# A gated encoder layer on one core: the FFN's row scale on the down product's sum, seven products in three accumulating chains, sums of weight blocks made by transfers that add

## The chip, the cores and the metric

The kernel runs on one core of a Trainium2 chip. The metric is the device time of one execution in microseconds (us); the runs before the change took 1766.96 to 1771.07, with a median of 1769.09. TensorE is called PE, VectorE DVE, ScalarE ACT, GpSimd POOL; SP issues most transfers.

## The reference, cut to what matters

The layer is computed for 1024 rows of a prompt and 32 rows of a sample with the same weights. Two attention mixers give `o_a` and `o_b`; then:

```python
def merge_and_ffn(x, o_a, o_b, gate_a, gate_b, w_branch_a, w_branch_b, w_out, g_ffn, w_up, w_down):
    pa = jnp.einsum('blc,cd->bld', o_a.reshape(B, L, WIDTH_A), w_branch_a)
    pb = jnp.einsum('blc,cd->bld', o_b.reshape(B, L, WIDTH_B), w_branch_b)
    m = jax.nn.sigmoid(gate_a) * pa + jax.nn.sigmoid(gate_b) * pb
    h = x + jnp.einsum('bld,de->ble', m, w_out)
    u = jnp.einsum('bld,df->blf', rmsnorm(h, g_ffn), w_up)
    return h + jnp.einsum('blf,fd->bld', jnp.square(jax.nn.relu(u)), w_down)
```

The model width is 1024, the FFN width 4096, everything is float32. `rmsnorm` divides a row by the root of its mean square (plus 1e-6) and multiplies by `g_ffn`. That divisor is one positive number for each row, so it can be applied before the relu, or, squared, after the down product.

## The kernel before, in words

All activations lie transposed: features on the 128 partitions, rows on the free axis. The 1056 rows are two groups: group one has rows 0 to 511 in one chunk of 512 columns, group two has rows 512 to 1055 in two chunks of 272. Each float32 operand is split into a high part in float32r (a cast on ACT) and the low rest (a subtraction on POOL or DVE), and a product is three matmuls (`three`): high by high, high by low, low by high.

A kernel written as one stream of operations is ordered by a planner (`Plan`). Each operation gets an estimated duration (`cost`), a rank (FAST 0, PREP 1, MAIN 2, FILL 3, SLOW 4) and its dependencies; the planner then steps through time and gives each engine the ready operation with the lowest rank and, within a rank, the earliest recorded one. The order on each engine's queue is fixed when the program is built; on the chip each engine runs its queue in order and waits on semaphores. FFN matmuls have rank FILL, the work that empties their PSUM banks FAST, the loading and splitting of weights PREP.

Weights come in units of 128 x 512 (four 128 x 128 blocks): a load into `wst`, the cast to `wh` on ACT, the subtraction to `wl` on POOL. Five `wh`/`wl` pairs are kept (`WB`).

The stages that matter here:

- `out` computes `h` block by block (`e`), scales it by `g_ffn` into the FFN's inputs `g.h` and `g.l`, adds up the squares in `g.acc`, and leaves `h` itself in `g.y`.
- `ffn_group` first turns `g.acc` into the row scale `rb2` (a matmul with ones to add over partitions, then `rsqrt` with a Newton step on DVE). 32 up blocks follow (`go_up`), in eight rounds `q` of four, each round followed by eight down blocks (`go_down(e, q)`), which are added to `g.y` block by block. The last up of a round comes one block early: four ups, among them the first of the next round, stand between two sets of downs.
- In group one an up block is one product of 24 matmuls of 512 columns, a down block one of 12. Ups and downs use the same ring of two PSUM banks (`pj`). Attention for later rows (`late`) runs beside the first half of group one's FFN.
- In group two an up step is a quad (`go_up_quad`): two up blocks by two column chunks, 2 x 2 x 2 products of half the depth, made with seven products (a Strassen-Winograd scheme) of 12 matmuls of 272 columns. Their operands are sums of quarters of the input (`quarters`) and of weight blocks (`quad_units`). The seven results lie in separate banks and are added on DVE. Group two has six `pj` banks for quads and two `pd` banks for downs.

After an up product the squared relu is made by DVE (`ru`: relu times the row scale, from PSUM to SBUF), POOL (`ru` squared), ACT (cast to `uh`, shown as `xh`) and DVE (the low part `ul`, shown as `xl`). The PSUM bank is free after the first of these.

The sums of weight blocks before, for blocks a11, a12, a21, a22 loaded into `raw` tiles:

```python
V.tensor_add(z, a21, a22)
s1 = part(z, w, "s", 4, V)
V.tensor_sub(a21, a11, a21)
V.tensor_sub(z, z, a11)
s2 = part(z, w, "s", 4, G)
s3 = part(a21, w, "s", 4, V)
V.tensor_sub(z, a12, z)
s4 = part(z, w, "s", 4, G)
```

All operations are recorded through one helper, so the profile shows one line (L408) for all; groups are told apart by tile names.

Of the kernel before, what the change touches and what calls it, by code (L numbers as in the profile page):

```python
# [19 lines left out]
D = 1024  # L20
# [82 lines left out]
class Plan:  # L103
# [115 lines left out]
    def cost(self, eng, op, out, ins, scalar, kw):  # L219
# [37 lines left out]
        if eng == ACT and op != "dma_start":  # L257
            d = 195 + 0.84 * n + (190 if "accum_out" in kw else 0)
            if op == "activation" and any(not isinstance(kw.get(k, 0.0), (int, float)) for k in ("scale", "bias")):
                d += 100  # L260
            return d - 90, d
        if eng == POOL:
            d = 300 + 0.9 * n if op in ("tensor_scalar", "memset") else 330 + 1.9 * n
            return d - 30, d
# [152 lines left out]
class Layer:  # L417
# [47 lines left out]
    def three(self, ps, wh, wl, xh, xl, first, last):  # L465

        mm = self.nc.tensor.matmul
        mm(ps, wh, xh, start=first, stop=False)
        mm(ps, wh, xl, start=False, stop=False)
        mm(ps, wl, xh, start=False, stop=last)  # L470

    def column_block(self, units, rhs, done, chunks, kn=KB, tag="pj"):

# [21 lines left out]
    def run(self):  # L495
# [23 lines left out]
        self.trir = c([128, 128], F32R, "trir")  # L519
        self.tri4r = c([128, DEC], F32R, "tri4r")  # L520
        self.gf = c([128, KB], F32, "gf")

        dt = lambda shape, name: nc.tile(self.dram, shape, F32, name)
        self.dq = dt([2 * H, 2, HD, T], "dq")
# [1 line left out]
        self.dv = dt([2 * H, 128, NT, 128], "dv")  # L526
        self.do = dt([2 * H, HD, T], "do")
        self.dg = dt([16, 128, T], "dg")

        self.wpool = nc.open("w")  # L530
        xp = nc.open("x")
# [112 lines left out]
    def constants(self):  # L644
        nc, a = self.nc, self.a
        for name, dst, n in (("tri", self.trir, 128), ("tri4", self.tri4r, DEC)):
            st = nc.tile(self.wpool, [128, 512], F32, name, tag="wst", bufs=3)
            nc.sync.dma_start(st[:, :n], a[name])
            nc.scalar.copy(dst, st[:, :n])
        nc.scalar.copy(self.identr, self.ident)  # L650
        nc.sync.dma_start(self.gf, a["g_ffn"])

    def normalise(self, sl):

# [665 lines left out]
    def out(self, g):  # L1320

        nc, a = self.nc, self.a
        for e in (0, 4, 1, 5, 2, 6, 3, 7) if g.i else range(KB):
            units = [self.unit(a["w_out"][e, j]) for j in range(2)]

            def done(c, cs, ps, e=e):
# [2 lines left out]
                    nc.sync.dma_start(xr, a["xT"][:, e, slice(g.lo + cs.start, g.lo + cs.stop)])  # L1329
                hv = g.y[:, e, cs]  # L1330
                nc.vector.tensor_add(hv, ps, xr)
                if g.i:
                    self.quarters(g, e, c, hv)
                if not g.i or c == 0 or e >= 4:
# [13 lines left out]
    def quarters(self, g, e, c, hv):  # L1348
# [32 lines left out]

    def quad_units(self, f):

        nc, a, w = self.nc, self.a, self.quads
        with nc.rank(PREP):
            raw = []
            for i, j in ((0, 0), (1, 0), (1, 1), (0, 1)):
                st = nc.tile(w, [128, 512], F32, "raw", bufs=10)
                nc.sync.dma_start(st, a["w_up"][f + i, j])
                raw.append(st)  # L1390
            a11, a21, a22, a12 = raw
# [9 lines left out]
            z = nc.tile(w, [128, 512], F32, "raw", bufs=10)  # L1401
            V.tensor_add(z, a21, a22)
            s1 = part(z, w, "s", 4, V)
            V.tensor_sub(a21, a11, a21)
            V.tensor_sub(z, z, a11)
            s2 = part(z, w, "s", 4, G)
            s3 = part(a21, w, "s", 4, V)
            V.tensor_sub(z, a12, z)
            s4 = part(z, w, "s", 4, G)
            p11 = part(a11, self.wpool, "w", WB, G)  # L1410
            p12 = part(a12, self.wpool, "w", WB, G)
            p22 = part(a22, self.wpool, "w", WB, G)
        return p11, p12, p22, s1, s2, s3, s4

    def ffn_group(self, g, late=iter(())):
        nc, a, i = self.nc, self.a, g.i
        rb2 = g.acc
        for c, cs in enumerate(g.chunks):
            ps = self.bank("pj")
            nc.tensor.matmul(ps[:, :g.n], self.ones, g.acc[c], start=True, stop=True)  # L1420
            with nc.rank(FAST):
                self.rsqrt(rb2[c], ps[:, :g.n], D, lambda n: g.tmp(n, "pb", 3))
        nq, us = DFF // 512, {}

        def go_up(f):
            units = [self.unit(a["w_up"][f, j]) for j in range(2)]
            us[f] = uh, ul = g.mh[:, f % 8], g.ml[:, f % 8]

            def done(c, cs, ps):
                r = g.tmp("ru", "pb", 3)  # L1430
# [5 lines left out]
            self.column_block(units, lambda k, cs: (g.h[:, k, cs], g.l[:, k, cs]), done, g.chunks)  # L1436

        def go_up_quad(f):

            a11, a12, a22, s1, s2, s3, s4 = self.quad_units(f)  # L1440
            for i in range(2):
                us[f + i] = g.mh[:, (f + i) % 8], g.ml[:, (f + i) % 8]
            n = g.n
# [3 lines left out]
            def product(w, xs):  # L1447
                ps = self.bank("pj")[:, :n]
                with nc.rank(FILL):
                    for k in range(4):  # L1450
                        ks = slice(k * 128, k * 128 + 128)
                        self.three(ps, w[0][:, ks], w[1][:, ks], *xs[k], k == 0, k == 3)
                return ps

            z = [nc.tile(self.op, [128, 2, n], F32, "part", tag="o32", bufs=4) for _ in range(2)]
            p1, u2, u3, u4 = z[0][:, 0], z[0][:, 1], z[1][:, 0], z[1][:, 1]
            add = nc.vector.tensor_add

            def done(i, c, ps):
                cs = slice(c * n, c * n + n)  # L1460
                uh, ul = us[f + i]
                r = g.tmp("ru", "pb", 3)
                nc.vector.scalar_tensor_tensor(r, ps, 0.0, rb2[c], op0=ALU.max, op1=ALU.mult)
                nc.gpsimd.tensor_mul(r, r, r)
                nc.scalar.copy(uh[:, cs], r)
                nc.vector.tensor_sub(ul[:, cs], r, uh.bitcast(F32)[:, cs])

            ps = product(a11, x(0, 0))
            with nc.rank(FAST):
                nc.scalar.copy(p1, ps)  # L1470
            p5 = product(s1, ta)
            ps = product(s2, tb)
            with nc.rank(FAST):
                add(u2, ps, p1)
                add(u4, p5, u2)
            ps = product(a12, x(1, 0))
            with nc.rank(FAST):
                add(ps, ps, p1)
                done(0, 0, ps)
            ps = product(s3, tc)  # L1480
            with nc.rank(FAST):
                add(u3, ps, u2)
                add(ps, ps, u4)
                done(1, 1, ps)
            ps = product(s4, x(1, 1))
            with nc.rank(FAST):
                add(ps, ps, u4)
                done(0, 1, ps)
            ps = product(a22, td)
            with nc.rank(FAST):  # L1490
                add(ps, ps, u3)
                done(1, 0, ps)
# [12 lines left out]
        done = 0  # L1505

# [114 lines left out]
```

## Time and profile before

| | us |
|---|---|
| median of three runs | 1769.09 |
| the three runs | 1766.96, 1769.09, 1771.07 |
| span of the profiled execution | 1767.0 |
| PE busy in the span | 1739.5 (98%) |
| DVE busy | 1175.5 (67%) |
| ACT busy | 932.7 (53%) |
| POOL busy | 1054.6 (60%) |

The profiled execution has no separately measured run time; its span goes from the first to the last instruction. The share of busy time is a mean over stages with different limits. Matmuls are pipelined, so a row of a matmul is longer than the distance from one to the next; that distance is read from a count in a stretch. Group one's FFN begins near 842 us and ends near 1295; group two's begins near 1391 and ends at 1764.

### The profile page before, as it was taken

The numbers are of one execution on the slowest core, as the hardware profiler recorded it, in microseconds if no ns is written. First come the engines' busy times: TensorE is split into PE (matmuls) and PEld (weight loads), VectorE is DVE, ScalarE is ACT, GpSimd is POOL, SyncE is SP. The second block draws the span as 40 slices with busy tenths as digits, with TensorE's granted clock in tenths as the row PEclk, the third lists the DMA queues.
The fourth block names the chain that finished last, engine by engine and source line by source line (L and its number), as shares of the span: only waits on it lengthen the run. The fifth ranks groups of instructions, "written<-read, shape, count | busy, mean of one in ns | idle before, by whom it ended". The sixth has DMA issues, their size and how long they took to land.

```text
span 1767.0 us, 32459 instructions
## 1 busy us (share of the span) xinstructions
PE 1739.5 (98%) x11394; PEld 1600.1 (91%) x11394; DVE 1175.5 (67%) x2427; ACT 932.7 (53%) x2007; POOL 1054.6 (60%) x901
## 2 busy tenths in 40 slices
PE   8999999999999999999999999999999999999999
PEld 7999999999899888888888888888899999999999
DVE  7555678999666645788975556333357897777764
ACT  7444598973255676766655545432236543333331
POOL 3623232435366574899875555675558986666663
PEclk9999999999999999999999999999999999999999
DMA  8244451544566668555254353433374333333312
GB/s 258 72 133 118 116 177 59 148 144 143 178 179 168 169 183 225 175 163 151 69 162 123 118 154 98 144 109 99 106 237 137 95 104 92 94 91 96 96 48 88
DMA packets 152851, 234.90 MB, mean 133 GB/s; under 512 B 27248, under 2 KB 54480, under 8 KB 152688
## 3 DMA queue, kind: packets, MB, share of 16 engines
q1 hardware_dynamic: 152256, 232.48, 45.8%
q8 instruction: 90, 1.47, 0.4%
q14 instruction: 73, 0.60, 0.1%
q10 hardware_dynamic: 432, 0.34, 0.1%
HBM read 182.58 MB, written 50.08 MB: 132 GB/s over the span
## 4 chain that ended last, share of the span: by engine, by line
PE 85%; DVE 6%; DMA 4%; POOL 3%; issue 1%; ACT 1%; SPq 0%; ACTq 0%; POOLq 0%; DVEq 0%
PE pj L408 53%; PE s L408 13%; PE pd L408 10%; PE t L408 4%; PE o L408 4%; DMA q<-dq 1%; POOL wl L408 1%; DVE xl L408 1%; DMA k<-dk 1%; DVE raw L408 1%; DVE acc L408 1%; DVE rw L408 0%; DMA o<-do 0%; SPq L408 0%; POOL acc L408 0%
## 5 line engine op out<-in xcount | busy, mean ns | idle before, releaser
L408 POOL TENSOR_TENSOR wl<-wst,wh 128x512 fp32r<-128x512 f32 x350 | 488.5, 1400 | 388.4 <-ACT wh L408 358.2
L408 PE MATMUL pj<-xh,wh 128*128 128x512 f32 (+1 forms) x1600 | 557.3, 348 | 0.6 <-DVE vt L408 0.3
L408 PE MATMUL pj<-xh,wl 128*128 128x512 f32 (+1 forms) x1600 | 557.4, 349 | 0.0
L408 PE MATMUL pj<-xl,wh 128*128 128x512 f32 (+1 forms) x1600 | 555.8, 348 | 0.0
L408 ACT CAST wh<-wst 128x512 fp32r<-128x512 f32 x350 | 216.8, 621 | 361.7 <-PE pj L408 222.0
L408 PEld LDWEIGHTS pj<-xh,wh 128*128 128x128 f32 x1600 | 301.1, 188 | 33.6 <-ACT xh L408 0.7
L408 PEld LDWEIGHTS pj<-xh,wl 128*128 128x128 f32 x1600 | 300.8, 188 | 32.7
L408 PEld LDWEIGHTS pj<-xl,wh 128*128 128x128 f32 x1600 | 301.0, 188 | 32.1
L408 PE MATMUL pd<-xh,wh 128*128 128x272 f32 x512 | 147.6, 288 | 2.0 <-DVE y L408 2.0
L408 PE MATMUL pd<-xl,wh 128*128 128x272 f32 x512 | 147.7, 288 | 0.0
L408 PE MATMUL pd<-xh,wl 128*128 128x272 f32 x512 | 147.6, 288 | 0.0
L408 DVE TENSOR_TENSOR xl<-ru,xh 128x272 fp32r<-128x272 f32 (+1 forms) x96 | 114.2, 1202 | 46.0 <-ACT xh L408 45.7
L408 DVE TENSOR_TENSOR tt<-t,tt 128x512 fp32r<-128x512 f32 (+2 forms) x168 | 100.2, 622 | 40.3 <-ACT tt L408 38.6
L408 DVE TENSOR_TENSOR_SCAN rem<-rem 128x896 f32<-128x896 f32 (+6 forms) x66 | 118.7, 1823 | 10.0 <-ACT rem L408 9.8
L408 POOL TENSOR_TENSOR p<-p,rem 128x895 f32<-128x895 f32 (+6 forms) x66 | 103.3, 1578 | 29.8 <-DVE rem L408 26.4
L408 ACT ACTIVATE junk<-score,cand 128x384 bf16<-128x384 f32 (+1 forms) x124 | 116.1, 936 | 9.3 <-DVE cand L408 7.0
L408 ACT CAST tt<-t 128x512 fp32r<-128x512 f32 (+2 forms) x168 | 84.8, 540 | 48.2 <-PE t L408 42.8
L408 DVE TENSOR_TENSOR y<-pj,y 128x512 f32<-128x512 f32 x72 | 49.6, 689 | 83.9 <-PE pj L408 83.8
L408 PE MATMUL s<-k,q 128*128 128x384 f32 (+5 forms) x384 | 95.7, 356 | 7.1 <-DMA k<-dk 2.5
L408 PE MATMUL s<-wl,xh 128*128 128x256 f32 (+1 forms) x360 | 101.8, 285 | 0.2 <-POOL wl L408 0.2
L408 PEld LDWEIGHTS o<-tt,v 128*128 128x128 f32 x640 | 93.0, 189 | 9.7 <-DVE tt L408 1.1
L408 PE MATMUL s<-wh,xh 128*128 128x256 f32 (+1 forms) x360 | 100.3, 286 | 0.9 <-DVE small L408 0.7
(245 smaller groups left out, 3963.6 us busy)
## 6 DMA issues: line engine op xcount, KB each, us to landing
wst<-w_down SPq DMA_DIRECT2D x128, 256.0 KB, 2.7
q<-dq SPq DMA_DIRECT2D x64, 256.0 KB, 5.2
wst<-w_up SPq DMA_DIRECT2D x64, 256.0 KB, 2.7
raw<-w_up SPq DMA_DIRECT2D x64, 256.0 KB, 2.8
k<-dk SPq DMA_DIRECT2D x48, 256.0 KB, 3.5
v<-dv SPq DMA_DIRECT2D x48, 256.0 KB, 3.7
wst<-w_g SPq DMA_DIRECT2D x42, 256.0 KB, 3.4
dv<-vs SPq DMA_DIRECT2D x32, 256.0 KB, 2.4
```

The lines of the kernel that those rows point to most:

```text
L408: fn(*args, **kw)
```

## The change

1. **Row scale.** `rb2` becomes the reciprocal of the mean square plus 1e-6, without root and Newton step, and is made behind the first up step (`scales`). The up products are no longer multiplied by it. After seven of the eight down rounds the sum in `g.y` is multiplied by `rb2` and `h` is added, both on POOL; the eighth round's product is multiplied by `rb2` on DVE and added. `h` is stored to DRAM by `out` (`dh`) and loaded back then (`hx`); the first down round is copied to `g.y` by ACT in place of an addition.
2. **Squared relu** (`square`): ACT relu from PSUM to SBUF, DVE product of the bank with it back into the bank, ACT cast from the bank, DVE subtraction from the bank.
3. **Quads.** The seven products run in three PSUM chains (px, pz, py) that go on accumulating after partial sums have been copied out by ACT (`keep`); signs of some operands are turned, with a negated `g_ffn` (`ngf`).
4. **Sums of weight blocks.** Four transfers a quad, issued by POOL, add a block from DRAM to a tile; a block can so be loaded more than once: nine transfers a quad in place of four. The low part of s2 moves from POOL to DVE. The planner counts 1000 ns for an issue on POOL.

The diff, cut to its core:

```diff
+        if op == "dma_start" and eng == POOL:
+            return 1000.0, 1000.0
...
+        nc.vector.tensor_scalar(self.ngf, self.gf, -1.0, None, op0=ALU.mult)
...  (out)
                 nc.vector.tensor_add(hv, ps, xr)
+                nc.sync.dma_start(self.dh[e, :, slice(g.lo + cs.start, g.lo + cs.stop)], hv)
...  (quarters)
+        neg = self.ngf[:, e:e + 1]
-            nc.scalar.activation(g.raw[-1][:, c * n:c * n + n], hv, AF.Copy, scale=gf)
-        def less(out, z):
-            nc.vector.scalar_tensor_tensor(out, hv, gf, z, op0=ALU.mult, op1=ALU.subtract)
+            nc.scalar.activation(g.raw[-1][:, c * n:c * n + n], hv, AF.Copy, scale=gf if e < 4 else neg)
+        def mix(out, by, op):
+            nc.vector.scalar_tensor_tensor(out, hv, by, out, op0=ALU.mult, op1=op)
-        less(t1, t1)
+        mix(t1, neg, ALU.subtract if e >= 4 else ALU.add)
-            less(t3, t3)
+            mix(t3, gf, ALU.subtract)
...  (quad_units)
+            def load(*blocks, out=None):
+                st = out
+                if out is None:
+                    st = nc.tile(w, [128, 512], F32, "raw", bufs=10)
+                    nc.sync.dma_start(st, src(*blocks[0]))
+                    blocks = blocks[1:]
+                for b in blocks:
+                    nc.gpsimd.dma_start(st, src(*b), accum_op=ALU.add)
+                return st
+            z = load((1, 0), (1, 1))
+            z3 = load((0, 0), (1, 0))
+            a11, a22, a12 = load((0, 0)), load((1, 1)), load((0, 1))
             s1 = part(z, w, "s", 4, V)
+            load((0, 0), out=z)
+            s2 = part(z, w, "s", 4, V)
+            load((0, 1), out=z)
+            s3 = part(z3, w, "s", 4, V)
             s4 = part(z, w, "s", 4, G)
...
+    def square(self, g, ps, uh, ul, sign=1.0):
+        nc = self.nc
+        r = g.tmp("ru", "pb", 3)
+        nc.scalar.activation(r, ps, AF.Relu, scale=sign)
+        nc.vector.scalar_tensor_tensor(ps, ps, sign, r, op0=ALU.mult, op1=ALU.mult)
+        nc.scalar.copy(uh, ps)
+        nc.vector.tensor_sub(ul, ps, uh.bitcast(F32))
...  (ffn_group)
-                self.rsqrt(rb2[c], ps[:, :g.n], D, lambda n: g.tmp(n, "pb", 3))
+        def scales():
+            for c in range(len(g.chunks)):
+                ps = self.bank("pj")
+                nc.tensor.matmul(ps[:, :n], self.ones, g.acc[c], start=True, stop=True)
+                with nc.rank(FAST):
+                    v = g.tmp("rv", "pb", 3)
+                    nc.vector.tensor_scalar(v, ps[:, :n], 1.0 / D, EPS, op0=ALU.mult, op1=ALU.add)
+                    nc.vector.reciprocal(rb2[c], v)
...  (go_up, done)
-                nc.vector.scalar_tensor_tensor(r, ps, 0.0, rb2[c], op0=ALU.max, op1=ALU.mult)
-                nc.gpsimd.tensor_mul(r, r, r)
-                nc.scalar.copy(uh[:, cs], r)
-                nc.vector.tensor_sub(ul[:, cs], r, uh.bitcast(F32)[:, cs])
+                              lambda c, cs, ps: self.square(g, ps, uh[:, cs], ul[:, cs]), g.chunks)
...  (go_up_quad)
+            px = product(a11, x(0, 0))
+            p1 = keep(px)
+            pz = product(s1, ta)
+            p5 = keep(pz)
+            product(s2, tb, px)
+            u2 = keep(px)
+            product(s4, x(1, 1), pz)
+            done(0, 1, pz, pz, u2)
+            py = product(a12, x(1, 0))
+            done(0, 0, py, py, p1)
+            product(s3, tc, px)
+            done(1, 1, self.bank("pj")[:, :n], px, p5)
+            product(a22, td, px)
+            done(1, 0, px, px)
...  (go_down, done)
-                nc.vector.tensor_add(g.y[:, e, cs], ps, g.y[:, e, cs])
-                if q == nq - 1:
-                    nc.sync.dma_start(self.o["yT"][:, e, slice(g.lo + cs.start, g.lo + cs.stop)], g.y[:, e, cs])
+                y = g.y[:, e, cs]
+                if q == 0:
+                    nc.scalar.copy(y, ps)
+                elif q < nq - 1:
+                    nc.vector.tensor_add(y, ps, y)
+                else:
+                    nc.vector.tensor_mul(ps, ps, rb2[c])
+                    nc.vector.tensor_add(y, ps, y)
+                    nc.sync.dma_start(self.o["yT"][:, e, slice(g.lo + cs.start, g.lo + cs.stop)], y)
+            if q == nq - 2:
+                for c, cs in enumerate(g.chunks):
+                    y = g.y[:, e, cs]
+                    with nc.rank(PREP):
+                        hx = nc.tile(self.op, [128, g.w], F32, "hx", tag="sg", bufs=3)[:, :n]
+                        nc.sync.dma_start(hx, self.dh[e, :, slice(g.lo + cs.start, g.lo + cs.stop)])
+                        nc.gpsimd.tensor_mul(y, y, rb2[c])
+                        nc.gpsimd.tensor_add(y, y, hx)
...
             go_up_quad(0)
+            scales()
             go_up_quad(2)
...
         go_up(0)
+        scales()
```

More of the change, by code (lines that the diff above doesn't have):

```diff
@@ L463, in rsqrt, with three @@
         nc.vector.tensor_mul(out, out, w)
-    def three(self, ps, wh, wl, xh, xl, first, last):
+    def three(self, ps, wh, wl, xh, xl, first, last, **kw):
         mm = self.nc.tensor.matmul
-        mm(ps, wh, xh, start=first, stop=False)
-        mm(ps, wh, xl, start=False, stop=False)
-        mm(ps, wl, xh, start=False, stop=last)
+        mm(ps, wh, xh, start=first, stop=False, **kw)
+        mm(ps, wh, xl, start=False, stop=False, **kw)
+        mm(ps, wl, xh, start=False, stop=last, **kw)
     def column_block(self, units, rhs, done, chunks, kn=KB, tag="pj"):
@@ L521, in run @@
         self.gf = c([128, KB], F32, "gf")
+        self.ngf = c([128, KB], F32, "ngf")
         dt = lambda shape, name: nc.tile(self.dram, shape, F32, name)
@@ L528, in run @@
         self.dg = dt([16, 128, T], "dg")
+        self.dh = dt([KB, 128, T], "dh")
         self.wpool = nc.open("w")
@@ L1385, in quad_units @@
         with nc.rank(PREP):
[L1386 to L1391, printed above, removed]
+            src = lambda i, j: a["w_up"][f + i, j]
+            def load(*blocks, out=None):
[7 more added lines that the diff above has]
+                return st
             def part(z, pool, tag, bufs, eng):
@@ L1400, in quad_units @@
             V, G = nc.vector, nc.gpsimd
-            z = nc.tile(w, [128, 512], F32, "raw", bufs=10)
-            V.tensor_add(z, a21, a22)
+            z = load((1, 0), (1, 1))
+            z3 = load((0, 0), (1, 0))
+            a11, a22, a12 = load((0, 0)), load((1, 1)), load((0, 1))
             s1 = part(z, w, "s", 4, V)
[L1404 to L1408, printed above, removed]
+            load((0, 0), out=z)
+            s2 = part(z, w, "s", 4, V)
+            load((0, 1), out=z)
+            s3 = part(z3, w, "s", 4, V)
             s4 = part(z, w, "s", 4, G)
@@ L1413, in quad_units @@
         return p11, p12, p22, s1, s2, s3, s4
+    def square(self, g, ps, uh, ul, sign=1.0):
[5 more added lines that the diff above has]
+        nc.vector.tensor_sub(ul, ps, uh.bitcast(F32))
     def ffn_group(self, g, late=iter(())):
         nc, a, i = self.nc, self.a, g.i
+        n = g.n
         rb2 = g.acc
[L1418 to L1421, printed above, removed]
-                self.rsqrt(rb2[c], ps[:, :g.n], D, lambda n: g.tmp(n, "pb", 3))
+        def scales():
[6 more added lines that the diff above has]
+                    nc.vector.reciprocal(rb2[c], v)
         nq, us = DFF // 512, {}
@@ L1427, in go_up @@
             us[f] = uh, ul = g.mh[:, f % 8], g.ml[:, f % 8]
-            def done(c, cs, ps):
-                r = g.tmp("ru", "pb", 3)
-                nc.vector.scalar_tensor_tensor(r, ps, 0.0, rb2[c], op0=ALU.max, op1=ALU.mult)
-                nc.gpsimd.tensor_mul(r, r, r)
-                nc.scalar.copy(uh[:, cs], r)
-                nc.vector.tensor_sub(ul[:, cs], r, uh.bitcast(F32)[:, cs])
-            self.column_block(units, lambda k, cs: (g.h[:, k, cs], g.l[:, k, cs]), done, g.chunks)
+            self.column_block(units, lambda k, cs: (g.h[:, k, cs], g.l[:, k, cs]),
+                              lambda c, cs, ps: self.square(g, ps, uh[:, cs], ul[:, cs]), g.chunks)
         def go_up_quad(f):
@@ L1442, in go_up_quad, with product @@
                 us[f + i] = g.mh[:, (f + i) % 8], g.ml[:, (f + i) % 8]
-            n = g.n
             ta, tb, tc, td = ([(th[:, k], tl[:, k]) for k in range(4)] for th, tl in g.sums)
             x = lambda j, c: [(g.h[:, 4 * j + k, c * n:c * n + n], g.l[:, 4 * j + k, c * n:c * n + n]) for k in range(4)]
-            def product(w, xs):
-                ps = self.bank("pj")[:, :n]
+            def product(w, xs, ps=None):
+                first = ps is None
+                if first:
+                    ps = self.bank("pj")[:, :n]
                 with nc.rank(FILL):
@@ L1451, in product @@
                         ks = slice(k * 128, k * 128 + 128)
-                        self.three(ps, w[0][:, ks], w[1][:, ks], *xs[k], k == 0, k == 3)
+                        self.three(ps, w[0][:, ks], w[1][:, ks], *xs[k], first and k == 0, k == 3, skip_group_check=True)
                 return ps
-            z = [nc.tile(self.op, [128, 2, n], F32, "part", tag="o32", bufs=4) for _ in range(2)]
-            p1, u2, u3, u4 = z[0][:, 0], z[0][:, 1], z[1][:, 0], z[1][:, 1]
-            add = nc.vector.tensor_add
@@ L1459, in done, with keep @@
-            def done(i, c, ps):
+            def keep(ps):
+                t = nc.tile(self.op, [128, g.w], F32, "part", tag="o32", bufs=4)[:, :n]
+                with nc.rank(FAST):
+                    nc.scalar.copy(t, ps)
+                return t
+            def done(i, c, out, ps, more=None):
                 cs = slice(c * n, c * n + n)
                 uh, ul = us[f + i]
[L1462 to L1492, printed above, removed]
+                with nc.rank(FAST):
+                    if more is not None:
+                        nc.vector.tensor_add(out, ps, more)
+                    self.square(g, out, uh[:, cs], ul[:, cs], -1.0 if i else 1.0)
+            px = product(a11, x(0, 0))
```

## The prediction

> **What bounds the kernel now.** I read the page first, then busy time by stretches, then the chain of waits, then groups of instructions.
>
> ```profile
> span 1767.0 us, 32459 instructions
> PE 1739.5 (98%) x11394; PEld 1600.1 (91%) x11394; DVE 1175.5 (67%) x2427; ACT 932.7 (53%) x2007; POOL 1054.6 (60%) x901
> PE 85%; DVE 6%; DMA 4%; POOL 3%; issue 1%; ACT 1%; SPq 0%; ACTq 0%; POOLq 0%; DVEq 0%
> ```
>
> TensorE (PE) is nearly always busy and carries 85% of the chain. The change removes no matmul, so it can only win time in which PE stands still. The stretches (start:end, length, then busy time and count of PE, PEld, DVE, ACT, POOL, granted clock, DMA share) say where that is.
>
> ```profile
> 842.00:1124.00 282.00, 281.39 (x1565) 244.74 (x1564) 184.42 (x376) 154.04 (x294) 166.18 (x126) 1.00 0.43 119
> 1127.00:1295.00 168.00, 168.00 (x743) 139.11 (x742) 52.34 (x62) 53.11 (x89) 107.01 (x85) 1.00 0.43 126
> ...
> 1360.00:1400.00 40.00, 39.63 (x308) 38.87 (x307) 32.38 (x39) 27.04 (x61) 40.00 (x40) 1.00 0.39 112
> 1400.00:1420.00 20.00, 17.66 (x128) 17.44 (x127) 20.00 (x34) 7.81 (x16) 14.20 (x13) 0.91 0.25 72
> 1420.00:1440.00 20.00, 19.19 (x146) 18.37 (x145) 19.57 (x34) 8.34 (x18) 16.75 (x14) 1.00 0.30 88
> 1440.00:1465.00 25.00, 24.11 (x192) 23.79 (x190) 25.00 (x38) 11.35 (x22) 21.37 (x18) 1.00 0.37 106
> 1465.00:1491.00 26.00, 25.57 (x201) 25.35 (x202) 17.82 (x34) 7.80 (x14) 14.85 (x14) 1.00 0.31 92
> 1491.00:1727.60 236.60, 236.60 (x1886) 236.60 (x1885) 165.78 (x299) 88.79 (x167) 160.01 (x136) 1.00 0.31 86
> 1727.60:1764.20 36.60, 36.08 (x288) 35.85 (x286) 14.36 (x29) 5.54 (x10) 11.40 (x10) 1.00 0.30 94
> ```
>
> From 1491 on, 1886 matmuls of 272 columns take 236.6 us, 0.1254 each without a gap: group two's FFN has nothing to win there. At that rate 1400 to 1491 holds 667 matmuls, 83.7 us of work in 91: **7.3 us are lost while group two's FFN opens** (3.9, 1.7, 0.9 and 0.8 by stretch), with DVE full. From 1127 to 1295 (group one's FFN alone, 512 columns) 743 matmuls take 168 us, 0.226 each: nothing is lost there either. The chain names the loss, and the clock adds to it:
>
> ```profile
> 1405.53 2.90 DVE acc L408 x2
> ...
> 1412.48 0.36 DVE ru L408
> 1412.84 0.04 issue
> 1412.88 8.07 PE pj L408 x50
> ...
> 1410.00:1413.00 3.00, 0.66 (x6) 0.44 (x5) 3.00 (x7) 0.03 (x1) 1.11 (x2) 1.00 0.31 70
> 1413.00:1416.00 3.00, 3.00 (x16) 3.00 (x17) 3.00 (x7) 1.69 (x4) 2.77 (x4) 0.61 0.38 120
> 1416.00:1419.00 3.00, 3.00 (x22) 3.00 (x21) 3.00 (x4) 1.03 (x3) 2.33 (x2) 0.82 0.48 163
> ```
>
> DVE works through the row scale (`acc`: reciprocal and Newton step) while all PSUM banks wait for `ru`, which multiplies by it. PE stops about 2.5 us, and the granted clock then is 0.61 and 0.82 for 6 us.
>
> **Part by part, group two.** Means are in ns, from 1491 to 1727.6:
>
> ```profile
> L408 POOL TENSOR_TENSOR wl<-wst,wh 128x512 fp32r<-128x512 f32 x43 | 56.2, 1307 | 66.0 <-ACT wh L408 66.0
> L408 DVE TENSOR_TENSOR xl<-ru,xh 128x272 fp32r<-128x272 f32 x41 | 49.9, 1235 | 4.5 <-ACT xh L408 4.5
> L408 DVE TENSOR_TENSOR y<-pd,y 128x272 f32<-128x272 f32 x81 | 33.7, 434 | 43.4 <-PE pd L408 43.4
> L408 POOL TENSOR_TENSOR ru<-ru 128x272 f32<-128x272 f32 x43 | 31.3, 736 | 0.9 <-DVE ru L408 0.9
> L408 POOL TENSOR_TENSOR sl<-raw,sh 128x512 fp32r<-128x512 f32 x20 | 30.3, 1515 | 0.0
> L408 DVE TENSOR_TENSOR raw<-raw 128x512 f32<-128x512 f32 x38 | 26.9, 708 | 0.3
> L408 ACT CAST sh<-raw 128x512 fp32r<-128x512 f32 x40 | 24.8, 620 | 12.3 <-PE pj L408 8.5 <-DVE raw L408 3.8
> L408 DVE TENSOR_TENSOR pj<-pj,part 128x272 f32<-128x272 f32 x43 | 18.8, 438 | 1.7 <-PE pj L408 0.7
> L408 ACT CAST xh<-ru 128x272 fp32r<-128x272 f32 x42 | 17.6, 418 | 8.1 <-POOL ru L408 8.0
> L408 DVE TENSOR_TENSOR sl<-raw,sh 128x512 fp32r<-128x512 f32 x20 | 16.3, 816 | 10.2 <-ACT sh L408 10.2
> L408 ACT COPY part<-pj 128x272 f32<-128x272 f32 x11 | 4.2, 379 | 0.0
> ```
>
> One period is a quad (84 matmuls) and four down blocks (96): 180 x 0.1254 = 22.6 us, 10.5 of them in that stretch. DVE has 15.8 us a period, ACT 8.5, POOL 15.3. After, on DVE: four weight sums go (4 x 0.708), PSUM additions fall from 7 to 3 (4 x 0.438), one split comes from POOL (+0.816), and the four low parts read PSUM beside one SBUF tile, like `y<-pd,y` (4 x (1.235 - 0.434) less): 15.8 - 2.8 - 1.8 + 0.8 - 3.2 = 8.8. On ACT: two more keeps (0.379) and four relus (like the 0.418 cast): 10.9. On POOL: 4 x 0.736 and 1.515 go, four transfer issues come: 10.8 + 4D. No row has an issue on POOL. I bound D by SP's issue below (0.33) and by POOL's own 1.5 us row; I take 1.3, the row of POOL's other work on such a tile: 16.0 of 22.6. Hidden; POOL binds only above D = 2.95.
>
> The sums become a chain: split s1, add, split s2, add, split s4. Each load lands after 2.8:
>
> ```profile
> raw<-w_up SPq DMA_DIRECT2D x64, 256.0 KB, 2.8
> L408 SPq DMA_DIRECT2D raw<-w_up x64: 327/328/543, 1299.2 to 1666.3; - x64
> DMA to landing us min/median/max: 2.5/2.8/6.5
> ```
>
> An adding transfer I bound by 2.5 and 6.5, and take 2.8, the median of the same 256 KB. Chain: 2 x (0.62 + 0.82) + 2 x (1.3 + 2.8) + 0.62 + 1.5 = 13.2 us, from the release of s1's buffer to s4 of the next quad. In steady state PE wants s4 one period and one product after that release, 22.6 + 1.5 = 24.1 us, so both adds together may be late by 11 us. In the opening, quad 2 follows quad 0 at once: 10.5 + 1.5 = 12.0. There the chain is 1.2 late, which a12 and s3 can fill (3 us), but POOL, in whose queue the adds stand, was full up to 1400 (40.00 of 40). What is queued behind a waiting add is POOL's splits of `wl`, and PE waits for those. So the opening: the scale moves behind quad 0 and shrinks to one reciprocal, nobody waits for it until the seventh down block; DVE falls well below full. I take back 5.3 of the 7.3 us and leave 2.0 for late adds (bounds: 0 and all 7.3).
>
> Hidden at nothing: the added stores and reloads of h (SP: 24 stores, 24 loads at 0.33; DMA share 0.25 to 0.43); 48 POOL operations on y, two for each of 24 pieces, in the seventh down block, where five weight buffers stand ahead and POOL had 66 us idle in the stretch shown; ACT's 24 copies for the first down block, five more 256 KB transfers a quad (4 + 4 x 256 KB a period become 9 + 4, a share of about 0.5); the one DVE operation that makes `ngf`; the sign changes, which replace operations one for one; group one's row scale, behind its first up, for which nobody waits. At the end one DVE multiplication stands before the last addition, which is exposed: **+0.45** (row `y<-pd,y`).
>
> **Part by part, group one.** Here ups and downs share two PSUM banks. Before, the bank of an up product was free after one DVE operation; after, it is read by relu, product, cast and subtraction. The step from the last up to the downs, alone on PE:
>
> ```profile
> 1191.85 0.62 ACT L408 CAST wh<-wst 128x512 fp32r<-128x512 f32 x1 [1.58 <-issue]
> 1192.03 0.69 DVE L408 SCALAR_TENSOR_TENSOR ru<-pj,acc 128x512 f32<-128x512 f32 x1 [0.31 <-PE pj L408]
> ...
> 1194.55 0.39 PE L408 MATMUL pj<-xh,wh 128*128 128x512 f32 x1
> ...
> 1194.75 0.69 DVE L408 TENSOR_TENSOR y<-pj,y 128x512 f32<-128x512 f32 x1 [2.03 <-PE pj L408]
> ...
> 1195.09 0.61 ACT L408 CAST xh<-ru 128x512 fp32r<-128x512 f32 x1
> ...
> 841.35 0.60 ACT L408 ACTIVATE p<-s 128x512 f32<-128x512 f32 x1
> ```
>
> The up ends at 1192.0; the first down runs in the other bank until 1194.55, where the second takes the up's bank. After: weight cast to 1192.47, relu (0.60) to 1193.07, product (0.69), cast (0.61), subtraction (0.69, a PSUM source) and 0.04 between engines: 1195.25. That is 0.7 late. If the planner rather runs the third down first, it waits for the first one's addition, 1194.75 + 0.69 + 0.05 = 1195.49: 0.95 late. I take 0.95. Between two ups there are 24 x 0.226 = 5.4 us, enough. The step comes eight times; four of them lie after 1124, without attention to fill in: **+3.8** (bounds 2.8 and 3.8). The other four lie beside attention: its matmuls fill some gaps, but DVE (184 of 282 us busy) and ACT put their own work between the four steps. Half price, 0.5 each: **+2.0** (bounds 0 and 6, a 1.5 us wait at each). POOL's squaring, which goes, lay off the path.
>
> **Sum.** -5.3 + 0.45 + 3.8 + 2.0 = +0.95 us on the profiled 1767.0, so 1768.0. The median of the runs, 1769.09, is 2.1 above that span; with the same distance: 1770.0. That is no change: 0.2% of this kernel, 3.5 us, is about what a measurement can tell.
>
> **Rivals.** *Faster*: the opening closes whole (-7.3), hand-overs cost only 0.7 (2.8) and nothing beside attention: -4.1, 1765.0; without any hand-over loss 1762.2. For it: DVE falls from 15.8 to 8.8. Against it: the second down needs the up's bank by construction. 27%.
>
> *Slower by held banks*: beside attention every step waits, 6 us: +5.0, 1774. It decides when those four steps cost over 4.6. For it: ACT and DVE are over half busy there. Against: attention has matmuls. 13%.
>
> *The opening stays shut*: adds and POOL's full queue take the place of the row scale, and 1 us is won, not 5.3: +5.2, 1774. For it POOL's 40.00 of 40; against it that the first two quads' blocks can be loaded far ahead (loads start at 1299). 9%.
>
> *POOL becomes the bound*: each 0.1 us of D above 2.95 costs 0.4 a period and 6 us over 15 periods; at 3.2, 1785. Against it: DVE's rows in the steady stretch are two-operand operations, which stretch POOL's own from 1307 to 1515 and no further. 7%.
>
> The Trainium skill, page SBUF — State Buffer, section SBUF: two separate sides, speaks for this last one: a transfer issued from GpSimd cannot get its descriptors written while VectorE runs a two-port mode, and one of about 0.62 us took 3.1. With D = 3.1, an estimate from that page, POOL would have 23.2 us a period and the kernel some 9 us more. No trace here shows such a transfer; the page ties the lock to copies and scalar operations, which the steady rows do not hold.
>
> The forecast itself holds the remaining 44%. Faster by over 0.2%: 27%; within: 44%; slower: 29%. The range, 1763.5 to 1778, cuts off POOL's case and the end of the faster one.
>
> **What would show it.** Right: 1400 to 1491 holds over 700 matmuls at clock 1.00; DVE near 8.8 a period; gaps near 0.9 at four steps from up to down after 1124, with PE waiting for DVE `xl` or `y`. Wrong: no such gaps; POOL over 20 us a period; an adding transfer landing after 9 us, with ACT `sh` waiting for it and PE for ACT.

## The result and the profile after

The changed kernel took **1786.16 us** (median; 1783.62 to 1789.47), the kernel before, run beside it, 1768.95. The ratio is 1.0098 [1.0083, 1.0113]: slower by 17 us. The forecast was 1770.0 in 1763.5 to 1778, so it was wrong, on the slow side.

The page of the changed kernel: span, busy engines, the software queue (packets, MB, share of 16 DMA engines), issues (KB, median us to landing), and the chain's shares.

```profile
span 1785.7 us, 32620 instructions
PE 1746.7 (98%) x11394; PEld 1601.3 (90%) x11394; DVE 1049.7 (59%) x2304; ACT 977.7 (55%) x2153; POOL 1026.9 (58%) x901
...
q0 software_dynamic: 9216, 16.78, 6.0%
...
PE 83%; DMA 5%; POOL 4%; DVE 4%; issue 2%; ACT 1%; SPq 0%; ACTq 0%; POOLq 0%; DVEq 0%
...
raw<-w_up POOLq DMA_DIRECT2D x64, 256.0 KB, 4.5
```

DVE lost 126 us of work and POOL 28, PE does the same 11394 matmuls, and the kernel is slower. The averages mislead: what counts is where PE stands still. I take that as **loss**: the length of a stretch less its matmuls at the spacing that they have without gaps. At 272 columns that is 0.1254 us, as counted in the prediction. For other widths I estimate (columns + 29)/2.4 ns from it, which gives 0.2254 us at 512, where 0.226 was counted, but take at least 0.108 us, the distance in runs of short matmuls, and four times as much for a row of the product with ones. The last is too much: two such rows and one matmul took 0.69 us at 1410.14, so a row takes 0.28, not 0.50, and the opening's losses are low by up to 0.9 us (by 0.4 in the kernel before). The table has us of the two profiled executions; its last stretch goes to 2.7 us before the end of the span, so it holds time behind the last matmul too.

| stretch | what runs | before | after | the steps summed to |
|---|---|---|---|---|
| 870 to 1124 | group one's FFN beside attention | 4.0 | 9.7 | +2.0 |
| 1124 to 1295 | group one's FFN alone | 0.6 | 6.4 | +3.8 |
| 1295 to 1395 | group two's branch and `out` | -0.3 | 3.0 | 0 |
| 1395 to 1495 | group two's FFN opens | 8.1 | 5.4 | -5.3 |
| 1495 to 1700 | group two's FFN, steady | 0 | 0 | 0 |
| from 1700 | its end | 0.6 | 6.9 | +0.45 |

The differences sum to 18.4 us; the spans differ by 18.7. Up to 780 us the change makes no difference of note (losses 40.3 and 40.8). By 1295 the changed kernel is some 12 us behind, so the same work lies later in it. Stretches of the changed kernel and then of the kernel before (columns as in the prediction; the last one is GB/s):

```profile
870.00:1124.00 254.00, 249.39 (x1378) 215.67 (x1377) 141.04 (x339) 142.19 (x271) 121.07 (x97) 1.00 0.44 122
1124.00:1295.00 171.00, 167.04 (x732) 136.40 (x731) 44.23 (x66) 61.51 (x105) 107.85 (x85) 1.00 0.42 122
1316.00:1326.00 10.00, 10.00 (x82) 10.00 (x81) 3.58 (x6) 2.94 (x5) 6.72 (x7) 1.00 1.03 302
1326.00:1336.00 10.00, 9.39 (x75) 9.17 (x74) 2.17 (x5) 3.45 (x6) 2.87 (x4) 1.00 1.08 313
1500.00:1700.00 200.00, 200.00 (x1596) 200.00 (x1595) 86.52 (x196) 90.69 (x197) 120.29 (x106) 1.00 0.67 150
1752.00:1757.00 5.00, 1.39 (x7) 0.95 (x6) 0.44 (x1) 0.00 (x0) 4.76 (x6) 0.93 0.11 28
1757.00:1760.00 3.00, 3.00 (x16) 3.00 (x15) 0.81 (x2) 0.62 (x1) 2.82 (x4) 0.54 0.54 143
```

```profile
870.00:1124.00 254.00, 253.47 (x1408) 220.86 (x1407) 157.42 (x352) 132.19 (x250) 145.94 (x115) 1.00 0.44 124
...
1306.00:1316.00 10.00, 10.00 (x82) 10.00 (x81) 10.00 (x12) 5.20 (x9) 6.46 (x5) 1.00 0.92 318
1316.00:1326.00 10.00, 10.00 (x82) 10.00 (x81) 5.42 (x13) 6.12 (x11) 7.39 (x7) 1.00 0.63 199
1326.00:1336.00 10.00, 10.00 (x82) 10.00 (x81) 5.62 (x11) 5.91 (x14) 9.27 (x11) 1.00 0.67 188
```

**Hand-overs in group one.** The timeline of the changed kernel at one of the four steps after 1124 (start, duration; in brackets the engine's idle time and what ended it):

```profile
1201.66 0.59 ACT L410 CAST xh<-pj 128x512 fp32r<-128x512 f32 x1 [0.77 <-DVE pj L410]
1202.25 0.39 PE L410 MATMUL pj<-xh,wl 128*128 128x512 f32 x1
1202.68 0.69 DVE L410 TENSOR_TENSOR y<-pj,y 128x512 f32<-128x512 f32 x1 [1.05 <-PE pj L410]
1203.29 0.68 DVE L410 TENSOR_TENSOR xl<-pj,xh 128x512 fp32r<-128x512 f32 x1
1203.42 0.50 PE L410 MATMUL pj<-xh,wh 128*128 128x512 f32 x1 [0.78 <-DVE y L410]
```

The up's bank is held by product, cast and subtraction (`xl`, until 1203.97), so PE turns to the other bank, which DVE's addition `y` releases: 0.94 more between two matmuls than their spacing. The four steps lose 0.95, 0.94, 0.94 and 1.03.

The largest stop beside attention, 1.86 us, is at a step of the same kind, from the last up of a round to its downs:

```profile
894.60 3.74 DVE L410 TENSOR_TENSOR_SCAN rem<-rem 128x1024 f32<-128x1024 f32 x1 [0.26 <-ACT rem L410]
...
899.45 0.59 ACT L410 COPY y<-pj 128x512 f32<-128x512 f32 x1
...
900.09 0.50 PE L410 MATMUL pj<-xh,wh 128*128 128x512 f32 x1 [1.70 <-ACT y L410]
```

The relu of the up's bank was done at 894.99, but DVE's product stands behind attention's scan `rem` and starts at 898.26; ACT's cast of the bank waits for the product, and behind the cast, in ACT's order, stands the copy `y` that frees the other bank for PE.

**The opening.** The chain of the changed kernel (start, us, what) no longer stops for the row scale's result near 1410, but twice later (`sh` and `sl` are the high and low part of a sum of weight blocks). Then DVE, POOL and ACT on the timeline:

```profile
1424.86 1.76 DVE acc L410
1426.91 2.21 DVE sl L410
1429.16 1.53 PE pj L410 x10
...
1442.92 0.88 POOL raw L410
1443.89 7.27 DMA raw<-w_up
...
1452.47 1.78 PE pd L410 x12
```

```profile
1424.18 0.68 DVE L410 TENSOR_TENSOR sl<-raw,sh 128x512 fp32r<-128x512 f32 x1
...
1426.83 2.27 DVE L410 TENSOR_TENSOR sl<-raw,sh 128x512 fp32r<-128x512 f32 x1
...
1425.72 2.83 POOL L410 TENSOR_TENSOR wl<-wst,wh 128x512 fp32r<-128x512 f32 x2
...
1451.23 0.62 ACT L410 CAST sh<-raw 128x512 fp32r<-128x512 f32 x1 [2.85 <-DMA raw<-w_up]
1452.03 0.39 ACT L410 COPY y<-pd 128x272 f32<-128x272 f32 x1
```

The first stop (2.13 us) is a split of a sum, `sl`, behind the reciprocal `acc` in DVE's order: the row scale still stands on this chain. The split takes 2.27 us in place of the 0.68 of the one before it, with two subtractions of POOL beside it until 1428.55. (The Trainium skill, page SBUF — State Buffer, section SBUF: two separate sides, calls the port pair that VectorE and GpSimd share an exclusive lock: an operation of VectorE with two SBUF inputs waits for the whole of one on GpSimd. The end of `sl` 0.55 us after POOL's agrees.) The second (1.71 us) is an adding transfer that lands after 7.27 us; ACT's cast `sh` waits for it, and behind that, in ACT's order, stands the copy of a down product whose bank PE needs. Two waits of the product with ones for POOL's sum of squares `acc`, at 1410 and 1415, take another 1.1 us (0.7 in the kernel before).

**The end.** PE and POOL of the changed kernel on the timeline:

```profile
1752.80 0.29 PE L410 MATMUL pd<-xl,wh 128*128 128x272 f32 x1
1756.42 0.60 PE L410 MATMUL pd<-xh,wl 128*128 128x272 f32 x1 [3.33 <-POOL wl L410]
...
1752.24 0.76 POOL L410 TENSOR_TENSOR y<-y,hx 128x272 f32<-128x272 f32 x1 [0.61 <-DMA hx<-dh]
1752.96 1.47 POOL L410 TENSOR_TENSOR y<-y,acc 128x272 f32<-128x272 f32 x2
1754.39 0.76 POOL L410 TENSOR_TENSOR y<-y,hx 128x272 f32<-128x272 f32 x1
1755.10 1.26 POOL L410 TENSOR_TENSOR wl<-wst,wh 128x512 fp32r<-128x512 f32 x1
```

Four operations on `y` stand ahead of the weight split `wl` for which PE waits 3.33 us, and the clock is 0.54 in the next 3 us (stretch above). In all 5.6 us are lost up to the last matmul; the rest of the 6.9 lies behind it, with the multiplication added there.

**The steady stretch** has no loss, as said: 1596 matmuls in 200.00 us.

### The profile page after: what moved, and what is told of

Same layout as the page of the kernel before. It is cut to its first block, busy times and chain, and to the rows that moved or that the text cites. A ratio compares the mean times of both kernels' runs of the same rounds, so it can differ in the third digit from the quotient of the medians.

```text
span 1785.7 us, 32620 instructions
## 1 busy us (share of the span) xinstructions
PE 1746.7 (98%) x11394; PEld 1601.3 (90%) x11394; DVE 1049.7 (59%) x2304; ACT 977.7 (55%) x2153; POOL 1026.9 (58%) x901
## 3 DMA queue, kind: packets, MB, share of 16 engines
q0 software_dynamic: 9216, 16.78, 6.0%
## 4 chain that ended last, share of the span: by engine, by line
PE 83%; DMA 5%; POOL 4%; DVE 4%; issue 2%; ACT 1%; SPq 0%; ACTq 0%; POOLq 0%; DVEq 0%
PE pj L410 51%; PE s L410 13%; PE pd L410 10%; PE t L410 5%; PE o L410 4%; POOL wl L410 2%; DMA sg<-dg 1%; DVE xl L410 1%; DMA raw<-w_up 1%; POOL y L410 1%; DMA q<-dq 1%; POOL xl L410 1%; POOL acc L410 1%; POOL pb L410 0%; SPq L410 0%
## 5 line engine op out<-in xcount | busy, mean ns | idle before, releaser
L410 POOL TENSOR_TENSOR wl<-wst,wh 128x512 fp32r<-128x512 f32 x350 | 483.4, 1389 | 390.4 <-ACT wh L410 365.4
L410 POOL TENSOR_TENSOR p<-p,rem 128x895 f32<-128x895 f32 (+6 forms) x66 | 99.2, 1516 | 32.2 <-DVE rem L410 29.8
L410 ACT CAST tt<-t 128x512 fp32r<-128x512 f32 (+2 forms) x168 | 84.7, 541 | 44.3 <-PE t L410 40.3
L410 PE MATMUL s<-wh,xl 128*128 128x256 f32 (+1 forms) x360 | 100.8, 283 | 0.0
L410 PE MATMUL o<-tt,v 128*128 128x256 f32 (+1 forms) x640 | 99.0, 278 | 1.4 <-DVE o L410 0.7
```

The costliest lines, as they stand in the source:

```text
L410: fn(*args, **kw)
```

## The experiments

Each ratio is to the kernel before, run beside it on the same chip, with its 95% interval.

**u1: the operations on y to DVE.**

```diff
-                        nc.gpsimd.tensor_mul(y, y, rb2[c])
-                        nc.gpsimd.tensor_add(y, y, hx)
+                        nc.vector.tensor_mul(y, y, rb2[c])
+                        nc.vector.tensor_add(y, y, hx)
```

> The changed kernel with the row scale of the sum and the addition of h moved from POOL to DVE. Theory P (48 operations on POOL, about 36 us, push the last weight splits back, and TensorE stops 3.5 us at 1752.8 and then runs at clock 0.54): the gap near the end and the one at 1267 in group one go, 5 to 7 us less than the changed kernel, so about 1780. Rival: the stop comes from late loads of weights or of h, then the gap stays and the time too (1786).

1782.5 us, 1.0069 [1.0057, 1.0081]: 5 us of the loss is back. At the end the loss falls from 6.9 to 3.6 (what is left are three waits for DVE's `y`, 1.29, 0.57 and 0.33 us, and the time behind the last matmul), and from 6.4 to 5.3 in 1124 to 1295, where the changed kernel had one wait of 0.89 at 1267 for POOL `wl` as well.

**u2: group one's up bank free after one operation.** Relu to SBUF as in the change, then the square on POOL, cast and subtraction from SBUF.

```diff
         nc.scalar.activation(r, ps, AF.Relu, scale=sign)
+        if not g.i:
+            nc.gpsimd.tensor_mul(r, r, r)
+            nc.scalar.copy(uh, r)
+            nc.vector.tensor_sub(ul, r, uh.bitcast(F32))
+            return
```

> The changed kernel, but in group one the squared relu works from the SBUF copy after ACT's relu (POOL squares, ACT casts, DVE subtracts), so the PSUM bank is free after one operation. Theory B (held banks): the four gaps of 0.95 after 1124 go, and most of the 5.8 us lost beside attention too: 6 to 9 us less, about 1778. Rival: the loss beside attention comes from another order of the attention work; then only the 3.8 us go, about 1782.

1778.41 us, 1.0043 [1.0026, 1.0060]. One edit takes 6.3 us out beside attention (9.7 to 3.4) and 4.0 after it (6.4 to 2.4); u2's stretch, to be held against the two above:

```profile
870.00:1124.00 254.00, 254.00 (x1415) 221.25 (x1414) 141.99 (x328) 144.24 (x276) 144.07 (x115) 1.00 0.43 124
```

So the held bank, with DVE's product on it, is the cause at both places, and beside attention it costs more than alone. Of the 2.4 left, 1.55 is one wait for POOL `wl`; in u2 the operations on y are still on POOL.

**u3: the sums of weight blocks on DVE again,** four loads a quad, s2's low part left on DVE.

```diff
-            z = load((1, 0), (1, 1))
-            z3 = load((0, 0), (1, 0))
-            a11, a22, a12 = load((0, 0)), load((1, 1)), load((0, 1))
+            a11, a21, a22, a12 = load((0, 0)), load((1, 0)), load((1, 1)), load((0, 1))
+            z = nc.tile(w, [128, 512], F32, "raw", bufs=10)
+            V.tensor_add(z, a21, a22)
+            V.tensor_add(a21, a11, a21)
+            z3 = a21
...
-            load((0, 0), out=z)
+            V.tensor_add(z, z, a11)
...
-            load((0, 1), out=z)
+            V.tensor_add(z, z, a12)
```

> The changed kernel with the sums of weight blocks made by DVE again (four additions of 128x512 a quad, four loads a quad), all else as in the changed kernel. Theory X (adding transfers cost: 7.3 us to land at 1443.9, ACT waits in order behind them, and their traffic slows the loads of group two's branch): losses at 1334, 1346 and 1450 go, 4 to 5 us less, about 1781.5. Rival (DVE relief by the transfers is worth more): DVE fills again in the opening, 2 to 4 us slower, about 1789.

1780.17 us, 1.0053 [1.0040, 1.0066]. The loss of 1295 to 1395 goes (3.0 to -0.1), the opening's falls from 5.4 to 3.6, now mostly one stop of 2.87 us for DVE's work on a bank of the quad (`pj`), after which the clock is 0.50 for 3 us. u3's stretches:

```profile
1316.00:1326.00 10.00, 10.00 (x82) 10.00 (x81) 5.99 (x12) 4.31 (x8) 4.83 (x4) 1.00 1.00 360
1326.00:1336.00 10.00, 10.00 (x82) 10.00 (x81) 6.29 (x11) 5.60 (x10) 6.69 (x6) 1.00 0.66 205
```

Here too the 16 DMA engines are full for ten us, but they move 360 GB/s and are through at 1326; in the changed kernel they move 302 and 313 and stay full until 1336. In the kernel before, 12 us earlier, they were 0.92 busy for ten us at 318 GB/s, with no loss.

**u4: the three together.**

> The three edits together: what is left of the change is the row scale on the sum, the three accumulating chains and, in group two, the squared relu in PSUM. If the three theories hold and add up: 1786 less 6, 8 and 4.5, about 1767; and since the opening's row scale is gone too, it may fall below the kernel before, to 1764. If they share one cause, it stays above 1772.

1765.84 us, 0.9978 [0.9970, 0.9987]: faster than the kernel before. The single edits took 0.0029, 0.0055 and 0.0045 off the ratio, 0.0129 in sum; together they take 0.0120. As far as the intervals tell, the three causes are separate and make up the whole loss; what is left of the change (scale on the sum, chains, group two's squared relu in PSUM) is a gain of 4 us.

**v1: u4, but the operations on y on POOL, recorded with the last rank.**

```diff
-                        nc.vector.tensor_mul(y, y, rb2[c])
-                        nc.vector.tensor_add(y, y, hx)
+                    with nc.rank(SLOW):
+                        nc.gpsimd.tensor_mul(y, y, rb2[c])
+                        nc.gpsimd.tensor_add(y, y, hx)
```

> As the kernel with all three edits (1765.8 against 1770.7 of the kernel before), but the 48 operations on y are on POOL again and ranked behind everything else there (SLOW in place of PREP); the loads of h keep their rank. If their place in POOL's queue was the fault: no stop near the end, nor the 2.2 us of gaps that DVE's operations on y make there, and 1.5 to 3 us less than with DVE, about 1763. Rival: POOL has not the time at all; then the stop of 3.5 us is back, about 1770.

1763.32 us, 0.9965 [0.9953, 0.9978]; loss from 1700 on: 1.1, against 3.6 in u4, and PE has no stop there (over all runs the intervals of v1 and u4 overlap). POOL has the time, here without the adding transfers; the rank PREP and the early place in the record put the work ahead of the splits.

**v2: u4 with 8 plain transfers more a quad,** of weights to memory that nobody reads.

```diff
+            for k in range(8):
+                nc.sync.dma_start(self.idle[f // 2 % 2 * 8 + k], src(k % 2, k // 2 % 2))
```

> As the kernel with all three edits, plus eight plain transfers of 256 KB a quad from the weights to an unused place in DRAM, issued by SP with the loads: about the time on the DMA engines that the adding transfers took, without POOL's issue, without a chain and without anyone who waits for them. If traffic is what the adds cost: late loads and gaps in group two's branch (2 to 4 us) as in the changed kernel, about 1769 to 1770. Rival (the chain and the waits behind it cost, not the traffic): within 1 us of 1765.8.

1820.74 us, 1.0287 [1.0271, 1.0302], and no answer: nothing held these transfers back, so all 128 went in one burst near 1296 to 1430 instead of a quad at a time. It shows only what full DMA engines do (v2's stretch; the loss is 30.8 and 26.9 us in the two stretches from 1295 to 1495):

```profile
1336.00:1356.00 20.00, 14.45 (x89) 13.79 (x88) 7.74 (x15) 6.57 (x13) 9.82 (x11) 0.83 1.02 362
```

**v3: u4, but seven banks added by DVE in place of the three chains.**

```diff
-            px = product(a11, x(0, 0))
-            p1 = keep(px)
-            pz = product(s1, ta)
-            p5 = keep(pz)
-            product(s2, tb, px)
-            u2 = keep(px)
...
+            ps = product(a11, x(0, 0))
+            with nc.rank(FAST):
+                nc.scalar.copy(p1, ps)
+            p5 = product(s1, ta)
+            ps = product(s2, tb)
+            with nc.rank(FAST):
+                add(u2, ps, p1)
+                add(u4, p5, u2)
...
```

> As the kernel with all three edits, but the seven products lie in seven banks and are added on DVE as before (seven additions of 272 columns a quad in place of three). If the chains save what DVE lacks in the opening: the gap at 1400 grows by some 2 us, about 1768. Rival: the steady stretch has room, and only the opening's few additions count: within 1 us of 1765.8.

1763.92 us, 0.9971 [0.9957, 0.9986]; u4's interval overlaps it. The stop for DVE `pj` that u4 has in the opening like u3 (2.86 us) is not there; the longest is 1.07.

**v4: the chains alone.** Row scale with root and Newton step ahead of the first up again, the relu times it, the square on POOL, no `dh`, sums on DVE.

```diff
-        nc.scalar.activation(r, ps, AF.Relu, scale=sign)
...
+        nc.vector.scalar_tensor_tensor(r, ps, 0.0, rb, op0=ALU.max if sign > 0 else ALU.min, op1=ALU.mult)
+        nc.gpsimd.tensor_mul(r, r, r)
...
+                    self.rsqrt(rb2[c], ps[:, :n], D, lambda n: g.tmp(n, "pb", 3))
...
```

> The accumulating chains alone: sums of weight blocks on DVE, the row scale by root and Newton step ahead of the FFN and multiplied in the relu, squares on POOL, no store of h, one addition at the end; all as before. If the row scale's chain on DVE is what opens the gap of 2.5 us and the low clock at 1410: that stays, and the time is the kernel before's less at most 2 us, 1768 to 1770. Rival (the chains relieve DVE enough): 1766 or less.

1768.28 us, 0.9992 [0.9982, 1.0002]: no measurable change. With v3 this says where the gain of u4 is from: not from the chains, but from the row scale on the sum or group two's squared relu in PSUM, which v3 has without chains and v4 leaves out. No run parts these two. The opening's loss in v4 is 6.6, near the 8.1 of before; in v3 it is 0.9, in u4 3.9.

**w1: the change with u1's and u2's edits; the transfers go on adding. w2: w1 with POOL's transfers copying** in place of adding, so that count, bytes, queue and dependencies stay; the sums of weight blocks are left out, so w2's output is another.

```diff
-                    nc.gpsimd.dma_start(st, src(*b), accum_op=ALU.add)
+                    nc.gpsimd.dma_start(st, src(*b))
```

> The changed kernel with both other faults mended (operations on y on DVE, early release of group one's banks), so that only the adding transfers stand between it and the kernel with all three edits (0.9978 of the kernel before). Theory: the adds cost 3 us in group two's branch and 2 to 5 in the opening, as the undoing of them alone gave 6 to 8: ratio 1.001 to 1.002, 1771 to 1774 where the kernel before takes 1770. Rival (the price of the adds stood only beside the other two faults): 0.998 to 0.999.

> As the run before it in this set, but POOL's transfers copy the block over the tile in place of adding it: same number, same queue, same waits, no addition (the sums of weight blocks are left out, so the output is another). If the adding form itself is what is dear (1.67 us on the sixteen DMA engines for 256 KB and 4.5 us to landing, against 0.9 and about 3 for plain loads): 2 to 4 us less than with adds. Rival (five more transfers a quad, POOL's issues and the chain): the same within 1 us.

w1: 1772.66 us, 1.0013 [1.0004, 1.0022]. w2: 1766.06, 0.9979 [0.9965, 0.9992], the ratio of u4, which has four loads a quad. So five more transfers a quad cost nothing on balance (w2 also has none of u4's four DVE additions a quad); that they add costs 0.0034, some 6 us. The losses fall from 2.6 to 0.1 in 1295 to 1395 and from 6.8 to 1.4 in 1395 to 1495. The page and the groups say what differs, w1 first (queue; issues with median us to landing; ns of an issue on POOL, min/median/max; a stretch):

```profile
q0 software_dynamic: 9216, 16.78, 6.0%
raw<-w_up POOLq DMA_DIRECT2D x64, 256.0 KB, 4.5
...
L410 POOL DMA_DIRECT2D raw<-w_up x64: 856/883/1194, 1301.9 to 1705.4; - x64
...
1316.00:1336.00 20.00, 18.84 (x148) 18.41 (x147) 11.03 (x17) 11.06 (x21) 14.48 (x15) 1.00 0.93 255
```

```profile
q0 software_dynamic: 5120, 16.78, 2.9%
raw<-w_up POOLq DMA_DIRECT2D x64, 256.0 KB, 3.4
...
L410 POOL DMA_DIRECT2D raw<-w_up x64: 536/559/749, 1303.4 to 1699.5; - x64
...
1316.00:1336.00 20.00, 20.00 (x161) 20.00 (x160) 11.90 (x18) 12.09 (x23) 15.09 (x16) 1.00 0.78 256
```

For the same 16.78 MB adding takes twice the DMA engines' time (6.0% against 2.9%) and 144 packets a transfer against 80, lands 1.1 us later and holds POOL 0.32 us longer. At 255 and 256 GB/s the engines are 0.93 busy in w1 and 0.78 in w2. (The Trainium skill, page DMA: Bandwidth & Descriptors, section Rules for kernel authors, says that an accumulating transfer reads its destination and writes it later; the doubled engine time fits that further read.) Which of the three, engine time, landing or issue, makes the 6 us isn't separated.

**w3: v1 and v3 together. w4: w3 with s2's low part on POOL again.**

```diff
-            s2 = part(z, w, "s", 4, V)
+            s2 = part(z, w, "s", 4, G)
```

> The two variants that were faster than the kernel with all three edits in one: operations on y last in POOL's queue, and seven banks in place of the chains. Of the change only the row scale on the sum and group two's squared relu in PSUM are left. If their gains add: the end loses 1 us in place of 3.6, the opening 1 in place of 4; 1760 to 1762 where the kernel before takes 1770 (ratio 0.9945). Rival (both gains are scatter, each interval reached to 0.998): 0.997.

> As the run before it, with the low part of s2 on POOL again, as in the kernel before. DVE has 0.8 us a period less, POOL 1.3 more. In the opening POOL is full: 0 to 2 us slower than with s2 on DVE. Rival: DVE is what the opening lacks, and it is up to 1 us faster.

w3: 1763.29 us, 0.9956 [0.9942, 0.9970]; w4: 1762.8, 0.9956 [0.9942, 0.9969]: alike, and faster than both kernels compared here, 7 us below the 1769.78 of before. The opening in u4 and w4, then the end in w4:

```profile
1395.00:1495.00 100.00, 97.29 (x760) 96.70 (x759) 67.13 (x116) 54.64 (x128) 48.76 (x38) 0.98 0.31 90
```

```profile
1395.00:1495.00 100.00, 98.50 (x778) 97.73 (x777) 73.82 (x132) 52.61 (x121) 62.26 (x46) 1.00 0.33 96
1700.00:1759.00 59.00, 58.35 (x466) 58.12 (x464) 29.49 (x70) 14.03 (x30) 44.22 (x48) 1.00 0.34 106
```

18 matmuls more in the same 100 us (0.9 lost against 3.9, counted as above), and 1.1 lost at the end. The 0.9 is w4's and v3's; w3's profile has 2.3 there, with the same time over the runs, so a difference of 1 to 2 us between single profiles says little by itself.

## Why the prediction was wrong, step by step

Two steps that were priced at nothing failed, and two terms had a wrong size.

- **Failed: "Hidden at nothing: 48 POOL operations on y".** The named cover, POOL's idle time and five weight buffers ahead, is there on average but not in order: POOL runs its queue as planned, and PREP work recorded earlier goes ahead of splits that are due. It cost 5.6 us at the end, the stop and the low clock behind it, and 0.89 in group one. (The stretch's other 0.7 is the exposed multiplication, put at 0.45.) u1 and v1 show it, v1 that order and not capacity is at fault.
- **Failed: "Hidden at nothing: five more 256 KB transfers a quad, a share of about 0.5".** I took bytes for engine time, and a share over the steady period for one over the stretch where two quads are loaded ahead. From 1500 to 1700 the share was 0.67 (0.48 in w2, where the transfers copy), and at 1316 to 1336 it was 1.03 and 1.08; there the branch's own loads come late. Waits in the changed kernel from 1300 to 1500, total, times and longest (`w_ba` is a branch's weights, `sg` its gates):

```profile
ACT sh L410 <- DMA raw<-w_up: 13.1, 10, 2.9
...
ACT wh L410 <- DMA wst<-w_ba: 9.8, 5, 4.4
...
DVE y L410 <- ACT sg L410: 8.1, 3, 6.1
```

  It cost 3.3 us before the FFN began. w2 corrects my reading of it: the plain transfers lose nothing there (0.1), the adding does.
- **Mis-sized: the opening, -5.3.** Only 2.7 came back, or 2.2 with the product with ones counted right. Nobody waits for the row scale's result any more, but it did not leave the path: it is two reciprocals of 1.84 us, one a chunk, not one, and the second stands ahead of the `sl` for which PE waits. The rest stands at two new places in order queues, `sl` on DVE and `sh` on ACT. The term "2.0 for late adds" took 2.8 us for a landing; the median was 4.5, the deciding one 7.27, above the bound of 6.5. DVE's and POOL's splits side by side were not in the sum. With the sums on DVE (u3) the opening loses 3.6, for another reason, the stop for DVE `pj`.
- **Mis-sized: hand-overs beside attention, +2.0.** The mechanism was right (u2), but no discount was due: 5.7, inside the bounds of 0 and 6 and near their top. The stops that can be told at these steps sum to 4.2 (0.41, 1.86, 0.94, 0.30 and 0.73); u2 takes 6.3 out of the stretch. The largest shows attention making the wait longer, by its scan on DVE, where the prediction had it fill the gap. ACT's copies for the first down round, hidden at nothing, are what PE waits for in this stop and in the second of the opening: they are short (0.59 and 0.39 us), but stand in ACT's order behind something late.
- **Right: hand-overs alone.** 0.95 each was foreseen, 0.94 to 1.03 measured, with the third down ahead and DVE `y` as the release. The stretch lost 5.8 more than before: 3.9 in these, 0.9 for POOL `wl`, and 1.0 in gaps too small to follow.
- **Right: the steady stretch.** DVE 86.52 of 200 us is 9.8 a period of 22.6 (8.8 foreseen), ACT 90.69 is 10.2 (10.9).
- **The rival "POOL becomes the bound" is refuted** though its time, 1785, was the measured one. POOL has 120.29 of 200 us, 13.6 a period, and an issue took 0.883, not 2.95 (group of the steady stretch, changed kernel: busy and mean ns, then idle time and its releasers):

```profile
L410 POOL DMA_DIRECT2D raw<-w_up x35 | 30.9, 883 | 28.4 <-DVE sl L410 23.5 <-PE pj L410 1.8 <-DMA raw<-w_up 1.7
```

  The 3.1 us that the prediction cited from the Trainium skill, page SBUF — State Buffer, section SBUF: two separate sides, is there the time of a transfer; taken for that of an issue, as the prediction did, it is seen nowhere: the longest issue of w1 took 1.194.
- **The rival "slower by held banks"** held as a mechanism (the stretch lost 5.7, the stops at the steps 4.2; it was to decide above 4.6), **"the opening stays shut"** by half. I gave each a chance by itself; that several came together was in none of them.

## What to carry to other kernels

Where work is put down as hidden, look at the queue in which it stands at the place where it is due, not at the engine's average: here a POOL 58% busy stopped PE for 3.33 us, and a later rank for that work, tried in v1 beside the other edits, left no such stop. A transfer that adds is to be costed in DMA engine time at twice its bytes, and against the busiest stretch, not the mean. A PSUM bank that alternates between two products should be freed by the first operation that reads it: three more readings of the bank cost 10 us here, and one more operation on POOL in SBUF was free once POOL did not carry the operations on y (u4 loses 0.7 from 1124 to 1295, the kernel before 0.6).

## What was not expected of the hardware

- Adding transfers took twice the DMA engines' time and 1.8 times the packets of plain ones from the same queue (6.0% against 2.9%, 144 against 80 a transfer of 256 KB), and an issue 0.883 us of POOL against 0.559.
- One stop of 3.33 us brought the granted clock to 0.54 for the next 3 us, and idle times of 2.70 us (u4, at 1403) to 0.51, of 2.22 (w1, at 1415) to 0.63 and 0.80 in two stretches of 3 us; 1.98 us (changed kernel, at 1429) left it at 1.00, as did the four of about 0.95.
- A DVE subtraction of two SBUF tiles went from 0.68 to 2.27 us while POOL subtracted beside it.
